# Half tiles from tile 57, one head folded by GpSimd, and three TensorE heads in the last row of a log-sum-exp kernel

## The chip, the cores and the metric

One core of a Trainium2 chip runs the program. The metric is the device time of one execution in microseconds (us), as the median of several runs; the profiled execution has a span from its first to its last instruction, which is about 2 us shorter than that time. All instants below are microseconds from the start of the span of the run named.

## The reference, cut to what matters

```python
def reference(x, bias):                       # x: 8 x 2048 x 2048 f32, bias: 8 x 256 f32
    x_heads = x.reshape(B, S, H, Dh).transpose(0, 2, 1, 3) + bias[None, :, None, :]
    x_tiled = np.repeat(x_heads, 2, axis=2)   # each row's result is stored twice
    mx = x_tiled.max(axis=-1, keepdims=True)
    return mx.squeeze(-1) + np.log(np.exp(x_tiled - mx).sum(axis=-1))
```

For each row and each of its 8 heads of 256 columns: add the head's bias, take the exponential, sum, take the logarithm.

## The kernel before

The input is read in 64 tiles of 2 MB; a tile holds two rows (k = 0, 1) of 2048 columns in each of 128 partitions, and nine tile buffers keep loads far ahead of the work. I call tile 62's two rows 62a and 62b. A head can be worked off in several ways, which a "mode" deals out:

- by TensorE and ScalarE ("pe" heads): a small matmul puts the bias into PSUM, a second one (identity times x, the "data matmul") adds x, and ScalarE takes exp and sums it in one instruction;
- by ScalarE and VectorE: exp of x alone, then VectorE multiplies by exp(bias) and sums;
- by GpSimd: it adds the bias before exp, or ("fold") multiplies by exp(bias) and halves the head three times, so that VectorE has only 32 columns left to sum.

In a mode, `pe` is the number of pe heads of a row, `g0` the first head to which GpSimd adds the bias (8: none), `fold` the number of folded heads. BULK, MIXED and PROMPT name modes of the code; PROMPT_F1 and PROMPT_F2 are PROMPT with one and two folded heads.

```python
MIXED = dict(pe=1, acc=1, g0=4, late=False, fold=0)
PROMPT = dict(pe=2, acc=2, g0=8, late=False, fold=0)
STAGES = [(0, (BULK,)), (50, (MIXED,)), (56, (MIXED, MIXED)), (61, (PROMPT, PROMPT)),
          (62, (PROMPT, PROMPT_F1)), (63, (PROMPT_F2, PROMPT))]   # two modes: the tile comes in halves
# ... cut ...
pairs = [pp.tile([P, 2 * MM], F32, name=f"pair{i}") for i in range(2)]   # PSUM, two banks each
ps = [p[:, c : c + MM] for p in pairs for c in (0, MM)]                  # four slots of one bank
# ... cut ...
def on_x(t, ins, after):
    known = [u for u in users[t] if u.ins.engine != ins.ins.engine]
    # ... cut: and the users of the same buffer's earlier tiles ...
    for u in known:
        if u not in after:
            tc.declare_no_dep(ins.ins, u.ins, reason="waited for by those it waits for")
    users[t].append(ins)
    return ins
# ... cut ...
            p = ps[n_ps[0] % len(ps)][:, 0 : (kb - ka) * n]   # put_bias: the next slot in turn
            n_ps[0] += 1
```

Slots are dealt in turn, two slots make one PSUM tile (a "pair"), and in the half-tile stages one half takes one slot. And `on_x` removes dependencies among the instructions that touch the same x tile. Waits are otherwise made by the build. ScalarE takes the pe heads of one half after it has issued the exp of the next half.

The softmax here doesn't subtract the row's maximum and nothing guards it: scores larger than these inputs give would overflow.

## Time and profile before

| the kernel before | |
|---|---|
| time | 327.51 us (327.42 to 327.84, 3 runs) |
| last piece of x has landed | 319.45 |
| VectorE's sums end | 322.00 |
| ScalarE's last head ends | 321.67 |
| span | 325.5 |

The way to read it is in the prediction. In all profile lines PE is TensorE, PEld its weight loads, DVE VectorE, ACT ScalarE and POOL GpSimd; L307 is line 307 of that run's kernel. The end of the load, in 1 us windows of the kernel before (the window, its length, busy time and number of instructions of PE, PEld, DVE, ACT and POOL, then the granted clock, that is the share of the full TensorE clock, the DMA share and GB/s):

```profile
319.00:320.00 1.00, 0.02 (x1) 0.00 (x0) 1.00 (x7) 1.00 (x3) 0.92 (x2) 1.00 0.99 295
320.00:321.00 1.00, 0.00 (x0) 0.00 (x0) 1.00 (x7) 1.00 (x6) 0.84 (x3) 1.00 0.45 152
```

TensorE is done at 319, VectorE and ScalarE are full: the tail belongs to them, and TensorE's clock happens to be 1.00 here.

### The profile page before, as it was taken

Reading aid. Unit: us, or ns where it says so; the run is one execution under the profiler, and the core shown is the slowest. Engines: PE = TensorE matmul, PEld = TensorE weight load, DVE = VectorE, ACT = ScalarE, POOL = GpSimd, SP = SyncE. Lnnn points to the kernel's source line nnn. Section 1 sums busy time; section 2 is a strip of 40 time slices with the busy share of each in tenths; the row PEclk is TensorE's granted clock in tenths of the full one; section 3 lists DMA queues with packets and bytes.
Section 4 is the critical chain, followed back from the end, with each engine's and each line's share of the span. In section 5 each row is a group of like instructions: output and inputs, shape, how many; then the busy total and the mean of one; then the engine's idle time right before and its main releaser. Section 6 shows DMA issues by size and latency. Waiting matters only on the chain.

```text
span 325.5 us, 2113 instructions
## 1 busy us (share of the span) xinstructions
PE 250.0 (77%) x541; PEld 86.9 (27%) x541; DVE 285.9 (88%) x320; ACT 264.3 (81%) x421; POOL 289.9 (89%) x88
## 2 busy tenths in 40 slices
PE   4478999499987888777879797889788455576792
PEld 1123333233322323223323232223223101122220
DVE  1006999999999999999898899989998999999995
ACT  1119999499978969888787978697879897799995
POOL 6999999799999999999999999999999999999713
PEclk9999999899979979998997989797979855555558
DMA  8999999999999999999999999999999999999994
GB/s 293 427 431 429 431 429 424 431 427 429 429 429 429 427 426 429 429 423 430 432 425 429 431 422 427 431 427 429 429 431 425 429 432 424 413 422 421 422 400 143
DMA packets 11806, 135.42 MB, mean 416 GB/s; under 512 B 1361, under 2 KB 1489, under 8 KB 2833
## 3 DMA queue, kind: packets, MB, share of 16 engines
q1 hardware_dynamic: 11696, 135.27, 98.6%
q8 instruction: 4, 0.07, 0.1%
q14 instruction: 8, 0.07, 0.0%
q10 hardware_dynamic: 2, 0.01, 0.0%
q0 software_dynamic: 96, 0.00, 0.0%
HBM read 134.23 MB, written 1.05 MB: 416 GB/s over the span
## 4 chain that ended last, share of the span: by engine, by line
DMA 48%; DVE 33%; ACT 8%; POOL 6%; PE 3%; issue 1%; SPq 0%; DVEq 0%
DMA xt<-in_x_dram 45%; DVE R L326 27%; ACT xt L307 6%; DVE xt L319 4%; POOL xt L301 4%; DMA b<-bparts 2%; PE pair L249 1%; PE one_ps L249 1%; DVE xt L342 1%; ACT xt L282 1%; DMA brow<-in_bias_dram 1%; ACT xt L267 1%; POOL brest L173 1%; POOL brest L171 1%; PE pair L203 0%
## 5 line engine op out<-in xcount | busy, mean ns | idle before, releaser
L301 POOL TENSOR_TENSOR xt<-xt,b_rep 128x2048 f32<-128x2048 f32 (+1 forms) x66 | 277.3, 4210 | 18.9 <-DMA xt<-in_x_dram 18.9
L326 DVE TENSOR_REDUCE R<-xt 128x14 f32<-128x3584 f32 (+1 forms) x56 | 208.1, 3716 | 2.6 <-ACT xt L307 0.9
L307 ACT ACTIVATE xt<-xt 128x2560 f32<-128x2560 f32 (+3 forms) x91 | 164.2, 1828 | 14.8 <-POOL xt L301 14.3
L249 PE MATMUL pair<-xt,ident 128*128 128x512 f32 x200 | 105.5, 654 | 0.0
L249 PE MATMUL one_ps<-xt,ident 128*128 128x512 f32 x100 | 61.0, 695 | 19.9 <-DMA xt<-in_x_dram 19.8
L267 ACT ACTIVATE xt<-pair 128x1024 f32<-128x1024 f32 x50 | 52.3, 1045 | 17.2 <-PE pair L249 15.8
L249 PEld LDWEIGHTS pair<-xt,ident 128*128 128x128 f32 x200 | 42.4, 212 | 56.0 <-issue 56.0
L319 DVE TENSOR_TENSOR xt<-xt,w_ps 128x512 f32<-128x512 f32 x50 | 34.0, 680 | 25.6 <-ACT xt L307 25.4
L233 PE MATMUL pair<-xt,ident 128*128 128x512 f32 (+1 forms) x44 | 34.0, 872 | 21.2 <-DMA xt<-in_x_dram 18.2
L260 ACT ACTIVATE xt<-one_ps 128x256 f32<-128x256 f32 x100 | 37.7, 394 | 8.1 <-PE one_ps L249 8.1
L203 PE MATMUL one_ps<-b,ones 3*128 3x512 bf16 x50 | 19.0, 381 | 17.9 <-ACT xt L260 11.8
L203 PEld LDWEIGHTS <-ones 3*128 3x128 bf16 x150 | 12.5, 92 | 65.7 <-issue 59.7
L203 PE MATMUL pair<-b,ones 3*128 3x512 bf16 x100 | 29.9, 378 | 0.0
L249 PEld LDWEIGHTS one_ps<-xt,ident 128*128 128x128 f32 x100 | 15.6, 197 | 41.3 <-DMA xt<-in_x_dram 34.1
L260 ACT ACTIVATION_READ_ACCUMULATOR xt<-one_ps 128x1 f32 x100 | 22.1, 221 | 0.0
L342 DVE CUSTOM_DVE_ANT_0 xt<-xt,one_ps 128x256 f32<-128x256 f32 x50 | 19.1, 414 | 0.3 <-ACT xt L307 0.3
L233 PEld LDWEIGHTS pair<-xt,ident 128*128 128x128 f32 x44 | 10.4, 294 | 29.6 <-DMA xt<-in_x_dram 19.7
L342 DVE CUSTOM_DVE_ANT_0 xt<-xt,w_ps 128x256 f32<-128x256 f32 x45 | 17.5, 417 | 0.0
L282 ACT ACTIVATE xt<-pair 128x256 f32<-128x256 f32 x34 | 12.5, 374 | 0.1
L326 DVE TENSOR_REDUCE R_last<-xt 128x4 f32<-128x1024 f32 x10 | 12.1, 1214 | 0.0
L218 PE MATMUL pair<-b,ones 3*128 3x512 bf16 (+1 forms) x22 | 10.2, 465 | 1.1 <-ACT xt L267 1.1
L358 POOL TENSOR_TENSOR xt<-xt,w_sb 128x256 f32<-128x256 f32 (+1 forms) x2 | 2.1, 1026 | 8.7 <-ACT xt L307 8.5
(38 smaller groups left out, 55.9 us busy)
## 6 DMA issues: line engine op xcount, KB each, us to landing
xt<-in_x_dram SPq DMA_DIRECT2D x56, 2048.0 KB, 29.9
xt<-in_x_dram SPq DMA_DIRECT2D x14, 1024.0 KB, 21.0
xt<-in_x_dram SPq DMA_DIRECT2D x5, 256.0 KB, 11.4
out_dram<-res SPq DMA_DIRECT2D x1, 896.0 KB, 7.3
xt<-in_x_dram SPq DMA_DIRECT2D x2, 384.0 KB, 16.5
out_dram<-res_last SPq DMA_DIRECT2D x1, 128.0 KB, 1.7
b<-bparts POOLq DMA_DIRECT2D x3, 1.5 KB, 6.5
brow<-in_bias_dram ACTq DMA_DIRECT2D x1, 8.0 KB
```

What stands on the lines that cost most here:

```text
L203: nc.tensor.matmul(p, lhsT=ones3, rhs=each_row(b3, h * Dh, Dh, K), start=True, stop=False,)
L218: nc.tensor.matmul(p, lhsT=ones3, rhs=each_row(b3, 0, n, kb - ka), start=True, stop=False,)
L233: mm = nc.tensor.matmul(p, lhsT=ident, rhs=xts[t % NBUF][:, ka:kb, 0:n], start=False, stop=True,)
L249: mm = nc.tensor.matmul(p, lhsT=ident, rhs=xts[t % NBUF][:, :, h * Dh : (h + 1) * Dh], start=False, stop=True,)
L260: act = nc.scalar.activation(out=xts[t % NBUF][:, k, 0:Dh], in_=got[0][:, k * Dh : (k + 1) * Dh], func=ACT.Exp, accum_out=sums[:, k, 0:1],)
L267: act = nc.scalar.activation(out=xts[t % NBUF][:, :, Dh : m["pe"] * Dh].rearrange("p k (h j) -> p h k j", j=Dh), in_=got[-1].rearrange("p ...
L282: act = nc.scalar.activation(out=xts[t % NBUF][:, k, c : c + Dh], in_=p[:, c : c + Dh], func=ACT.Exp, accum_out=sums[:, k, h : h + 1],)
L301: add = nc.gpsimd.tensor_tensor(out=v, in0=v, in1=each_row(b_rep, c - G0, D - c, k1 - k0), op=ALU.add)
L307: return on_x(t, nc.scalar.activation(out=v, in_=v, func=ACT.Exp), [after])
L319: mul = nc.vector.tensor_tensor(out=f, in0=f, in1=each_row(w_ps, m["pe"] * Dh - W0, n, k1 - k0), op=ALU.mult,)
L326: red = nc.vector.tensor_reduce(out=sums[:, k0:k1, h0:H], in_=v.rearrange("p k (h j) -> p k h j", j=Dh), op=ALU.add, axis=mybir.AxisListTy ...
L342: ttr = nc.vector.tensor_tensor_reduce(out=v, in0=v, in1=w, scale=1.0, scalar=0.0, op0=ALU.mult, op1=ALU.add, accum_out=dst,)
```

## The change

The intent: fewer, cheaper half tiles (from 57 instead of 56, with GpSimd folding one head instead of adding a bias to four), BULK kept up to tile 53 instead of 49, less ScalarE work in tile 62, and in the very last row one head more for TensorE, so that VectorE has five sums in that row instead of six. The third TensorE head is loaded next to last, so that the last piece is one head of 128 KB.

```diff
-PROMPT = dict(pe=2, acc=2, g0=8, late=False, fold=0)
+SINGLE_F1 = dict(pe=1, acc=1, g0=8, late=False, fold=1)
+TRIPLE = dict(pe=3, acc=3, g0=8, late=False, fold=0)
 # ... cut ...
 STAGES = [
     (0, (BULK,)),
-    (50, (MIXED,)),
-    (56, (MIXED, MIXED)),
-    (61, (PROMPT, PROMPT)),
-    (62, (PROMPT, PROMPT_F1)),
-    (63, (PROMPT_F2, PROMPT)),
+    (54, (MIXED,)),
+    (57, (PROMPT_F1, PROMPT_F1)),
+    (62, (SINGLE_F1, SINGLE_F1)),
+    (63, (PROMPT_F2, TRIPLE)),
 ]
 LAST_COLS = [
     [(0, 512), (1280, 2048), (512, 1280)],
-    [(0, 512), (512, 1024), (1024, 1536), (1536, 2048)],
+    [(0, 512), (768, 1280), (1280, 1792), (512, 768), (1792, 2048)],
 ]
```

The rest of the diff (cut) lets a row have more than 512 TensorE columns, and lets heads go with any piece. One order of instructions changes with it: ScalarE now takes the two TensorE heads of 63a before the exps of 63b (`if c0 == 0: flush(for_pe)`), where the kernel before left them to the end.

More of the change, by code (lines that the diff above doesn't have):

```diff
@@ L211, in put_bias, with add_x @@
         n = m["pe"] * Dh
-        step = MM // n
+        rows = min(k1 - k0, max(MM // n, 1))
         got = []
-        for ka in range(k0, k1, step):
-            kb = min(ka + step, k1)
-            p = ps[n_ps[0] % len(ps)][:, 0 : (kb - ka) * n]
-            n_ps[0] += 1
-            nc.tensor.matmul(
-                p,
-                lhsT=ones3,
-                rhs=each_row(b3, 0, n, kb - ka),
-                start=True,
-                stop=False,
-            )
-            got.append((ka, kb, p))
-        return got
-    def add_x(m, t, k0, got):
-        n = m["pe"] * Dh
-        rows = []
-        for ka, kb, p in got:
+        for k in range(k0, k1, rows):
+            for c in range(0, n, MM):
+                w = min(n - c, MM)
+                p = ps[n_ps[0] % len(ps)][:, 0 : rows * w]
+                n_ps[0] += 1
+                nc.tensor.matmul(
+                    p,
+                    lhsT=ones3,
+                    rhs=each_row(b3, c, w, rows),
+                    start=True,
+                    stop=False,
+                )
+                got.append((k, k + rows, c, w, p))
+        return got
+    def add_x(m, t, k0, c0, c1, got):
+        heads = []
+        for ka, kb, c, w, p in got:
+            if not c0 <= c < c1:
+                continue
             mm = nc.tensor.matmul(
@@ L235, in add_x @@
                 lhsT=ident,
-                rhs=xts[t % NBUF][:, ka:kb, 0:n],
+                rhs=xts[t % NBUF][:, ka:kb, c : c + w],
                 start=False,
@@ L239, in add_x @@
             )
-            on_x(t, mm, [loads[t, k0, 0]])
-            rows += [(p[:, k * n : (k + 1) * n], mm) for k in range(kb - ka)]
-        return rows
+            on_x(t, mm, [loads[t, k0, c0]])
+            for i in range(0, (kb - ka) * w, Dh):
+                k, cw = divmod(i, w)
+                heads.append((ka + k, (c + cw) // Dh, p[:, i : i + Dh], mm))
+        return heads
     def late_heads(m, t, got, sums):
@@ L276, in late_heads, with sum_biased @@
         return pe_part
-    def sum_biased(m, t, k, p, mm, sums):
-        for h in range(m["pe"]):
-            c = h * Dh
-            act = nc.scalar.activation(
-                out=xts[t % NBUF][:, k, c : c + Dh],
-                in_=p[:, c : c + Dh],
-                func=ACT.Exp,
-                accum_out=sums[:, k, h : h + 1],
-            )
-            last_uses[t].append(on_x(t, act, [mm]))
+    def sum_biased(t, k, h, p, mm, sums):
+        act = nc.scalar.activation(
+            out=xts[t % NBUF][:, k, h * Dh : (h + 1) * Dh],
+            in_=p,
+            func=ACT.Exp,
+            accum_out=sums[:, k, h : h + 1],
+        )
+        last_uses[t].append(on_x(t, act, [mm]))
     def each_row(src, c, n, k_rows):
@@ L452, with pe_part @@
             add = None
+            heads = []
             if c0 == 0:
-                if m["late"]:
-                    pe_part = late_heads(m, t, bias_there, sums)
-                else:
-                    got = add_x(m, t, k0, bias_there)
+                bias_here = bias_there
+            if m["late"]:
+                pe_part = late_heads(m, t, bias_here, sums)
+            else:
+                heads = add_x(m, t, k0, c0, c1, bias_here)
+                def pe_part(t=t, heads=heads, sums=sums):
+                    for k, h, p, mm in heads:
+                        sum_biased(t, k, h, p, mm, sums)
+            if c0 == 0:
                 if next_units and not m["late"]:
@@ L461 @@
                     add = g_add(m, t, k0, k1)
-            if c0 == 0 and (t < T - 1 or k0 == 0):
-                flush(for_pool)
+                if t < T - 1 or k0 == 0:
+                    flush(for_pool)
             if t == T_PROMPT and c0 == 0:
@@ L475 @@
                     for_pool.append(fold(t, k0, hf, h1, sums, done))
-            if c0 == 0 and (t < T - 1 or k0 == 0):
+            if c0 == 0:
                 flush(for_pe)
@@ L493, in pool_part @@
                     load(t + NBUF)
-            if not m["late"]:
-                def pe_part(t=t, m=m, got=got, k0=k0, k1=k1, sums=sums):
-                    for k in range(k0, k1):
-                        sum_biased(m, t, k, *got[k - k0], sums)
             for_pool.append(pool_part)
-            if c0 == 0:
-                if m["g0"] < H:
-                    pe_part()
-                    if m["late"]:
-                        bias_there = put_bias(*next_units.pop(0))
-                else:
-                    for_pe.append(pe_part)
+            if m["g0"] < H:
+                pe_part()
+                if m["late"]:
+                    bias_there = put_bias(*next_units.pop(0))
+            elif heads:
+                for_pe.append(pe_part)
         fb, at = divmod(t - 2, NBLK)
```

## The prediction

> **What bounds the kernel now.** I read the page's shares and slices first, then the chain of waits for the last 30 us, then the timelines of TensorE and ScalarE for the same stretch.
>
> ```profile
> PEclk9999999899979979998997989797979855555558
> DMA  8999999999999999999999999999999999999994
> GB/s 293 427 431 429 431 429 424 431 427 429 429 429 429 427 426 429 429 423 430 432 425 429 431 422 427 431 427 429 429 431 425 429 432 424 413 422 421 422 400 143
> ```
>
> The DMA row is full in every slice but the first and the last: the kernel streams 134.2 MB at about 429 GB/s, and that stream sets the time. The chain's total (DMA 48%, VectorE 33%) must not be read as "VectorE is a third of the bound": it follows VectorE only through the early tiles, where VectorE works off the start-up backlog while transfers run full beside it. The completion events of the trace give the pace: a 2 MB tile lands every 4.90 us, a half tile every 2.48 us, the first half of tile 62 at 311.74, its second at 314.24, the seven pieces of tile 63 from 314.91 to 319.45. Nothing in the change moves these bytes. So what it can touch is what comes after the last landings: 319.45 to the span's end, 325.5, about 6.1 us. This is how that end looks in the chain of waits:
>
> ```profile
> 294.41 19.82 DMA xt<-in_x_dram
> ...
> 314.26 1.48 ACT xt L307
> 315.74 1.46 ACT xt L282 x8
> 317.20 1.47 ACT xt L307 x2
> ...
> 318.69 0.42 DVE xt L342
> ...
> 321.86 0.14 DVE R_last L372
> 322.00 0.14 issue
> 322.14 0.32 PE tpair L408
> 322.45 0.02 issue
> 322.48 0.39 ACT res_last L414
> ```
>
> The columns are start, length, what. From the landing of tile 62's second half, ScalarE works without a gap: its exp (1.48), four bias heads (1.46), the two exps of tile 63's first row (1.47). Then VectorE does nine multiply-and-sum instructions, 3.09 us at 0.343 us each, and one small reduction, to 322.00. Transpose, Ln, store and the end take the other 3.5 us and stay. ScalarE's own last bias head ends at 321.67, so it is only 0.33 us off the path.
>
> TensorE looks idle enough on average, but not in clock. PEclk is 5 from 258 us to 316 us. The timeline of TensorE shows what this costs:
>
> ```profile
> 304.33 1.22 PE L233 MATMUL pair<-xt,ident 128*128 128x256 f32 x2 [0.94 <-DMA xt<-in_x_dram]
> ...
> 309.36 2.08 PE L233 MATMUL pair<-xt,ident 128*128 128x512 f32 x2
> 311.37 0.60 PE L218 MATMUL pair<-b,ones 3*128 3x512 bf16 x1
> 311.90 2.08 PE L233 MATMUL pair<-xt,ident 128*128 128x512 f32 x2
> ...
> 316.52 1.13 PE L233 MATMUL pair<-xt,ident 128*128 128x512 f32 x2
> ```
>
> A pair of heads of one row (512 columns) takes 2.08 us at half clock and 1.13 us at full. With its bias matmul the period is 2.54 us (309.36 to 311.90), just more than the 2.48 us of a half tile.
>
> **What the Trainium skill says.** "TensorE: Matmul & The Clock Gate", Part 1: the array's clock is halved by default, and released only after a busy window of about 3.4 us that runs free of the kernel. The trace agrees: the granted clock is 0.5 or 1.0 alone, and the slow pieces last 3.41 us or multiples of it. The trace adds a grade: the window 309.07 to 312.49, in which the data matmuls filled 2.67 of 3.41 us, did not release the clock, the next, with 2.94, did (at 315.9). "DMA: Bandwidth & Descriptors", "Where 436 GB/s comes from", sets the ceiling at 435 GB/s and says that HBM binds near 358; the trace's 429 agrees with the first and not with the second. The same page, "Why small descriptors are slow (HBM only)", has a fixed cost per packet; here 2048-byte packets took 84 ns, and the last store's 1024-byte ones 46 ns, so two of those cost 8 ns more. "ScalarE: Activation LUTs", "Step-by-step: what each stage is for", has 0.833 ns per element: 1536 elements then are 1.28 us, and the trace has one such exp every 1.37 us with its start.
>
> **The change part by part.**
>
> 1. Tiles 50 to 53 go from MIXED back to BULK. VectorE per tile: 0.60 + 3.89 = 4.5 us against 4.35 us (six times 0.344 and a 2.28 us reduction), both under 4.90. Hidden: 0.
>
> 2. Tile 56 is loaded whole again, and 57 to 61 change from MIXED halves to PROMPT_F1 halves. Per half, before: GpSimd 2.33 us (add of 1024), ScalarE 2.3 us, VectorE 3 x 0.344 + 1.22 = 2.25. After: GpSimd 2.05 us (the fold in the trace, 315.82 to 317.87), ScalarE 1.37 + 2 x 0.365 = 2.1, VectorE 5 x 0.344 + 0.19 = 1.9. All under 2.48 and lower than before. There is a bump at the change-over: tile 56 lands at 284.4, its add lasts 4.56 us, its second exp comes at 289.1, and ScalarE is then behind by two halves. At 0.38 us regained per half (2.48 - 2.1) it is level again at tile 62, by my step-by-step addition at 311.7 us, VectorE at about 313.4. It is just in time, and the stream does not notice, since loads were issued 20 us earlier. Hidden: 0.
>
> 3. Tile 62 goes from PROMPT to SINGLE_F1: one bias head, seven exps, one folded. ScalarE per half: 1.37 + 256 x 0.833 ns + 0.365 = 1.95. VectorE: six instructions and a reduction, 2.25.
>
> 4. Row 1 of tile 63: three heads by TensorE, five by VectorE instead of six; heads 2 and 7 come as separate 128 KB pieces, head 7 last. Smaller packets: 2 x 8 packets per engine x 4 ns = 0.06 us later.
>
> The end of ScalarE and VectorE, added up from 314.26 with these durations: ScalarE exp of 62b 1.60 to 315.85, two heads to 316.58, two exps of 768 to 318.04 (before 318.67), two heads of row 0 to 318.77, exps of 512, 512 and 256 to 320.10. VectorE: 62a from 313.5 to 315.8, 62b from 316.0 (exp end) to 318.3, then nine instructions and a reduction, 3.31 us: 321.6. Before 322.0. So these two **gain 0.4 us**: the removed sixth instruction of the last row is paid for by the sixth in tile 62's second half.
>
> TensorE now. Tile 62 has only 256 columns per half, 1.22 of 2.48 us, so nothing in it would release the clock. At half clock: 62b 314.26 to 315.4, bias to 315.95, row 0 of tile 63 to 317.96 (its data lay there since 314.91), two bias matmuls to 318.83, heads 0 and 1 of row 1 (landed 317.54) to 320.9, head 2 another 1.2 us, to 322.1. ScalarE's last head then runs 322.1 to 322.55, against 322.0 for the end of the sums before: **a loss of 0.55 us**. At full clock the same work takes half and ends under ScalarE's exps; then VectorE's 321.6 stands.
>
> So the sum is -0.4 or +0.55 us, by the clock. I stepped the TensorE work through 3.41 us windows at forty phases, with release at 2.75 to 2.85 us of data matmul and fall below 2.2 to 2.33 us of all work (read from the windows before, as the rule above): the clock is low at the end in two thirds to four fifths of them. Weighted: about +0.3 us.
>
> **The rivals.** (a) The clock is at full rate at the end: PROMPT_F1 fills TensorE (2.54 of 2.48 us), which before released the clock after nine us of it (306.8 to 315.9). For: five tiles of it. Against: at full clock the load is only 1.5 of 2.48 us, and windows with 2.1 to 2.3 us of work were followed by a fall in the bulk stage; and tile 62 lies between. Time: 327.1. (b) TensorE at half clock becomes the bound of the tail: as worked out, 328.1, my main case. (c) The change-over backlog is not worked off by tile 62, because folds on GpSimd and sums on VectorE slow each other, or ScalarE's starts cost more: each tenth of a microsecond per half makes one microsecond at tile 62, and the end goes to 328.5 to 329. Against: VectorE's instructions kept 0.343 us in the trace while GpSimd folded (316 to 321). (d) The extra pieces or the store of the first seven batches (896 KB, 314.3 to 321.64) get in the way of the last loads: it is issued after the piece eight earlier has landed, so now 0.7 us later than before; that helps by at most 0.1 us.
>
> **Range and chances.** From 327.51: 327.1 with a quarter to a third of the weight, 328.1 with most of the rest, so 327.8. Run-to-run spread of the kernel before is 0.4 us; with (c) the range is 326.9 to 328.6. Two per cent is 6.5 us, more than the whole tail, and a lost stream would need an engine above 2.48 us per half for long: same 0.98.
>
> **What would show it right or wrong.** DMA at about 429 GB/s up to slice 38 and the last piece landing within 0.3 us of 319.5 (step 0). VectorE's last small reduction at about 321.6 (sum of the tail). The data matmul of head 2 ending near 322 at clock 0.5, with the transpose waiting for ScalarE (main case), or near 320 at clock 1.0, with the transpose waiting for VectorE (rival a). ScalarE level with the landings at tile 62 (step 2). I am wrong if the stream itself shows a gap between 285 and 312, if the tail is bound by neither, or if the time moves by over a microsecond.

## The result and the profile after

The changed kernel takes **328.63 us** (328.42 to 328.90, 4 runs) against 327.67 us (327.42 to 327.94) of the kernel before in the same rounds: 0.96 us slower, ratio 1.0030, interval 1.0012 to 1.0047.

The stream did what was expected. The slices of the page of the changed kernel:

```profile
PEclk9999999879997997997997979798998997559657
DMA  8999999999999999999999999999999999999993
GB/s 296 428 431 431 429 429 422 429 427 431 425 427 431 427 424 431 423 433 426 426 431 427 427 428 423 427 433 423 427 433 424 425 433 419 421 421 421 419 384 97
```

The DMA row is as full as before, and by the completion events the last piece lands at 319.30, 0.15 us earlier than before. So the loss lies behind it. PEclk shows one difference: in the half-tile stage the clock is no longer low throughout (a 9 and a 6 among the 5s), but it is low towards the end, where it was high before. The chain of waits of the changed kernel, for the same stretch as in the prediction:

```profile
294.09 20.02 DMA xt<-in_x_dram
...
314.15 1.22 PE pair L237 x2
315.37 0.54 PE pair L220
315.90 2.02 PE pair L237 x2
317.92 0.02 issue
317.94 0.47 ACT xt L286 x2
318.42 1.46 ACT xt L311 x2
319.88 0.73 ACT xt L286 x4
320.61 0.53 ACT xt L311
...
321.16 0.42 DVE xt L346
...
322.96 0.14 DVE R_last L376
323.11 0.14 issue
323.24 0.32 PE tpair L412
```

Before, the chain went from the landing of 62b straight to ScalarE. ScalarE's exp of 62b still starts at once (314.13), but the chain now leads over three TensorE pieces: 62b's data matmul, the bias matmul of 63a, and 63a's data matmul, 3.8 us at half clock. ScalarE waits for them before its next head (0.47), and its exps of tile 63 come after it. The timeline of ScalarE says which head that is:

```profile
315.73 0.37 ACT L286 ACTIVATE xt<-pair 128x256 f32<-128x256 f32 x1
...
317.94 0.38 ACT L286 ACTIVATE xt<-pair 128x256 f32<-128x256 f32 x1 [1.76 <-PE pair L237]
```

The head at 315.73 is 62a's, the one at 317.94 is 62b's: tile 62 has one TensorE head per half. 62b's own data matmul had ended at 315.37. ScalarE stood 1.76 us for a matmul whose result it did not read.

The built program shows why. TensorE counts up a semaphore, and 62b's head waits for a value of it (read from a build of each kernel; no trace holds these values):

```
kernel           62b's head waits for   that value is reached by
changed          375                    63a's data matmul
e1_nodep         373                    62b's own data matmul
e2_align         377                    the bias matmul of 63b's third head
```

62b and 63a stand in the two banks of the same pair. The build keeps dependencies by PSUM tile, here a whole pair, and 63a's matmul is issued before 62b's head is, so the head waits for it. In the kernel before, the two halves that share a pair belong to the same tile, and there `on_x` happens to declare this dependency away. Starting the half tiles at 57 instead of 56 shifts the slots by one, and pairs now straddle two tiles.

### The profile page after: what moved, and what is told of

Its sections match the earlier page's. It is cut to its first block, busy times and chain, and to the rows that moved or that the text cites. A ratio compares the mean times of both kernels' runs of the same rounds, so it can differ in the third digit from the quotient of the medians.

```text
span 326.6 us, 2184 instructions
## 1 busy us (share of the span) xinstructions
PE 260.4 (80%) x565; PEld 90.3 (28%) x565; DVE 283.7 (87%) x306; ACT 263.6 (81%) x425; POOL 290.6 (89%) x123
## 4 chain that ended last, share of the span: by engine, by line
DMA 47%; DVE 34%; ACT 6%; POOL 6%; PE 5%; issue 1%; SPq 0%; DVEq 0%
DMA xt<-in_x_dram 44%; DVE R L330 29%; ACT xt L311 5%; DVE xt L323 4%; POOL xt L305 4%; DMA b<-bparts 2%; PE pair L255 2%; PE pair L237 1%; PE one_ps L255 1%; DMA brow<-in_bias_dram 1%; ACT xt L273 1%; ACT xt L286 1%; DVE xt L346 1%; POOL brest L171 1%; POOL brest L173 1%
## 5 line engine op out<-in xcount | busy, mean ns | idle before, releaser
L305 POOL TENSOR_TENSOR xt<-xt,b_rep 128x2048 f32<-128x2048 f32 x57 | 258.8, 4543 | 18.9 <-DMA xt<-in_x_dram 18.9
L330 DVE TENSOR_REDUCE R<-xt 128x14 f32<-128x3584 f32 (+1 forms) x56 | 214.5, 3830 | 1.9
L311 ACT ACTIVATE xt<-xt 128x2560 f32<-128x2560 f32 (+5 forms) x77 | 158.3, 2066 | 11.2 <-POOL xt L305 10.8
L255 PE MATMUL pair<-xt,ident 128*128 128x512 f32 x216 | 115.7, 663 | 0.0
L255 PE MATMUL one_ps<-xt,ident 128*128 128x512 f32 x108 | 65.8, 693 | 20.3 <-DMA xt<-in_x_dram 20.3
L237 PE MATMUL pair<-xt,ident 128*128 128x512 f32 (+1 forms) x36 | 28.6, 896 | 8.9 <-DMA xt<-in_x_dram 4.5
L346 DVE CUSTOM_DVE_ANT_0 xt<-xt,w_ps 128x256 f32<-128x256 f32 x61 | 22.4, 413 | 1.2 <-ACT xt L311 1.1
L370 POOL TENSOR_TENSOR xt<-xt 128x128 f32<-128x128 f32 (+3 forms) x39 | 13.9, 356 | 3.1
L362 POOL TENSOR_TENSOR xt<-xt,w_sb 128x256 f32<-128x256 f32 (+1 forms) x13 | 10.0, 773 | 6.6 <-ACT xt L311 6.0
L346 DVE CUSTOM_DVE_ANT_0 xt<-xt,one_ps 128x256 f32<-128x256 f32 x27 | 10.5, 411 | 0.9 <-ACT xt L311 0.9
```

The costliest lines, as they stand in the source:

```text
L237: mm = nc.tensor.matmul(p, lhsT=ident, rhs=xts[t % NBUF][:, ka:kb, c : c + w], start=False, stop=True,)
L255: mm = nc.tensor.matmul(p, lhsT=ident, rhs=xts[t % NBUF][:, :, h * Dh : (h + 1) * Dh], start=False, stop=True,)
L305: add = nc.gpsimd.tensor_tensor(out=v, in0=v, in1=each_row(b_rep, c - G0, D - c, k1 - k0), op=ALU.add)
L311: return on_x(t, nc.scalar.activation(out=v, in_=v, func=ACT.Exp), [after])
L330: red = nc.vector.tensor_reduce(out=sums[:, k0:k1, h0:H], in_=v.rearrange("p k (h j) -> p k h j", j=Dh), op=ALU.add, axis=mybir.AxisListTy ...
L346: ttr = nc.vector.tensor_tensor_reduce(out=v, in0=v, in1=w, scale=1.0, scalar=0.0, op0=ALU.mult, op1=ALU.add, accum_out=dst,)
```

## The experiments

**Theory A:** ScalarE is held by a false wait through the shared PSUM pair, and TensorE's half clock makes that wait long. **Rivals:** B, TensorE at half clock bounds the tail by itself; C, VectorE's additional sum in 62b; D, the later start of the half tiles and its backlog.

| run | time, us | before in its rounds | ratio (interval) |
|---|---|---|---|
| e1_nodep | 327.44 | 327.35 | 1.0000 (0.9988 to 1.0013) |
| e2_align | 329.33 | 327.35 | 1.0060 (1.0047 to 1.0072) |
| e3_before57 | 328.27 | 327.35 | 1.0034 (1.0021 to 1.0047) |
| e4_before58 | 328.37 | 327.35 | 1.0032 (1.0019 to 1.0046) |
| e5_warm | 326.96 | 327.47 | 0.9985 (0.9974 to 0.9997) |
| e6_nodep_warm | 326.94 | 327.47 | 0.9987 (0.9975 to 0.9999) |
| e7_before_odd | 328.15 | 327.47 | 1.0034 (1.0014 to 1.0053) |
| e8_nodep_2h | 327.49 | 327.47 | 0.9999 (0.9987 to 1.0011) |
| e9_before57_nodep | 327.93 | 327.45 | 1.0015 (1.0003 to 1.0027) |
| e10_nodep_62p | 328.34 | 327.45 | 1.0016 (1.0002 to 1.0031) |
| e11_before_warm | 327.44 | 327.45 | 1.0000 (0.9987 to 1.0013) |

All eleven gave correct results; the medians are of 5 runs (6 for e7 and e10).

### e1_nodep: the wait removed

```diff
             on_x(t, mm, [loads[t, k0, c0]])
+            x_mms.append(mm)
...
+        for other in x_mms:
+            if other is not mm and x_mms.index(other) > x_mms.index(mm):
+                tc.declare_no_dep(act.ins, other.ins, reason="another bank")
         last_uses[t].append(on_x(t, act, [mm]))
```

The head's wait for its own matmul stays.

> The changed kernel, with one false dependency declared away: a bias head's exp on ScalarE no longer waits for a later piece's data matmul that writes the other bank of the same PSUM pair. Theory A (that wait holds ScalarE 1.76 us, from 316.2 to 317.9 of the span): the head of tile 62's second half starts at about 316.1, the sums end near 322.0 instead of 323.1, time falls by 0.9 to 1.1 us to 327.5 to 327.7. Rival B (TensorE at half clock bounds the tail by itself, the wait is only where it shows): the end stays within 0.3 us of 328.6. Rival C (the added sixth sum per half of tile 62 loads VectorE): no change, 328.6.

Measured: 327.44 us, level with the kernel before. That is 1.19 us less than the changed kernel's median, or 0.87 us less if each is taken against the kernel before in its own rounds (328.63 - 327.67 = 0.96 and 327.44 - 327.35 = 0.09). Theory A's number holds. The chain of waits of this run:

```profile
314.09 1.22 PE pair L238 x2
315.32 0.53 PE pair L221
315.85 2.01 PE pair L238 x2
317.86 0.75 PE pair L221 x2
318.61 2.02 PE pair L238 x2
320.62 0.02 issue
320.65 0.84 ACT xt L288 x4
```

62b's head now starts at 316.03, as soon as ScalarE is free for it:

```profile
316.03 0.38 ACT L288 ACTIVATE xt<-pair 128x256 f32<-128x256 f32 x1
```

The tail is TensorE's at half clock, from the landing of 62b straight through, and the sums end with ScalarE's third head at 321.98. So B is real as a floor (it is why nothing is gained on the kernel before), but it was not what made the loss. C falls: VectorE's extra sum is still there.

### e2_align: slots shifted back

```diff
         n = m["pe"] * Dh
+        if k0 == 0 and k1 == 1 and n_ps[0] % 2:
+            n_ps[0] += 1
```

> The changed kernel with one PSUM slot skipped at tile 57, so that the two halves of a tile share a pair again, as in the kernel before. Theory A in its exact form (a head waits for whatever was last issued into its pair before it): tile 62's second head now shares its pair with nothing of tile 63's first row, but the third head of the last row (256 columns) falls on the other bank, so by the built program it waits for that bias matmul, which follows the data matmul of 63a: start at 318.5 instead of 317.9, so 0.5 to 0.7 us slower than the changed kernel: 329.1 to 329.4. Rival A' (only a pair that straddles two tiles hurts, aligned ones don't): 327.6. B and C: 328.6.

Measured: 329.33 us, 1.98 us over the kernel before in its rounds. This is the strange number that only the exact form of A expects: aligning the pairs makes it worse, since 63b with three heads takes two slots and the second falls into the pair of 62b. The timeline of ScalarE in this run:

```profile
318.62 0.39 ACT L288 ACTIVATE xt<-pair 128x256 f32<-128x256 f32 x1 [2.50 <-PE pair L222]
```

62b's head waits 2.50 us, for a bias matmul of the last row. Neither B nor C has a reason for that.

### e3_before57 and e4_before58: the start of the half tiles alone

In the kernel before, `(56, (MIXED, MIXED))` becomes `(57, ...)` in one run and `(58, ...)` in the other.

> The kernel before with half tiles from tile 57 instead of 56 and nothing else, which shifts its PSUM slots by one, so that pairs straddle two tiles. Theory A: the heads of tile 62's second half wait for the data matmul of tile 63's first row: 1.2 us later at full clock (317.65 instead of 316.4), 2.5 us at half clock; time 328.7 to 330.0. Rivals B and C, and 'the start of the half tiles costs nothing by itself': 327.7 within 0.3.

> The kernel before with half tiles from tile 58: pairs aligned again, two tiles fewer in halves. Theory A: 327.7 within 0.3, as the kernel before. Rival D (it is the later start of the half tiles, and the backlog at the change-over, that costs): slower than with 57, over 328.7.

Measured: 328.27 and 328.37 us. Neither lies in a range that I had given: e3 is slower, as A says, but by less than A's least (328.7), and e4 is above A's 328.0 and below D's 328.7. With 58 the pairs are aligned, and yet it is 1.0 us slower than the kernel before. So the later start costs something by itself, which A does not give; the direction is D's. The chain of e4 goes from the last whole tile to the end on VectorE:

```profile
289.26 4.55 POOL xt L301
...
293.83 1.92 ACT xt L307
...
295.77 2.29 DVE R_last L326
```

From there it does not leave VectorE until the last sum. A whole tile's late GpSimd add leaves VectorE behind, and MIXED halves (one every 2.15 us on VectorE, where the prediction had summed 2.25, per 2.48 us of load) regain too little per half. So in the kernel before, starting the halves at 56 and not at 58 is worth a microsecond for a reason of its own, and e3 may mix two causes.

### e9_before57_nodep: splitting e3

The kernel of e3 with the declaration of e1.

> Splits the run of the kernel before with half tiles from 57 (0.9 us slower) into its two possible causes: false wait or backlog of the change-over. The same kernel with the false dependency declared away. If the false wait was the cause (theory A): back to 327.4 to 327.7. If the backlog on VectorE was (as the run with 58 shows one): stays at 328.1 to 328.4.

Measured: 327.93 us, with single runs from 327.49 to 328.51, while e3's ran from 328.18 to 329.38. It lies between the two expectations, and the ranges overlap: by the medians the false wait makes perhaps a third of a microsecond of e3's 0.9. The two profiled executions (328.18 us for e3, 327.55 us for e9) say more. In e3's, 61b's first head stands for 62a's data matmul:

```profile
314.21 0.39 ACT L282 ACTIVATE xt<-pair 128x256 f32<-128x256 f32 x1 [0.86 <-PE pair L233]
```

In e9's, the same head starts at 313.22, and the chain stays on VectorE from the last whole tile to the last sum, as in e4. The sums end at 322.68 in e3's and 322.07 in e9's (322.00 in the kernel before). In this pair the wait makes 0.6 us, and the backlog alone leaves about 0.1. The other runs of e9, up to 328.51, have no profile, so how the medians divide stays open.

### e7_before_odd: the false wait put into the kernel before

```diff
         n = m["pe"] * Dh
+        if k0 == 0 and k1 == 1 and n_ps[0] % 2 == 0:
+            n_ps[0] += 1
         step = MM // n
```

> The kernel before with one PSUM slot skipped at tile 56, nothing else: same stages, same loads, pairs now straddle tiles. Theory A: heads of 61b and 62b wait for the next tile's data matmul, 0.9 to 2.5 us of ScalarE idle in all near 313 to 318, time 328.3 to 329.8. Rival (slots don't matter; the half-tile start and its backlog do): 327.4 within 0.2.

Measured: 328.15 us (327.86 to 330.08), 0.68 us slower than the kernel before, with the same stages and the same loads. Direction as A expects, size just below its range: in the profiled execution (328.09 us) the clock went to full at 313.74, so only one wait was long, that of 61b's heads for 62a's data matmul:

```profile
314.04 0.39 ACT L284 ACTIVATE xt<-pair 128x256 f32<-128x256 f32 x1 [0.67 <-PE pair L235]
```

This is the cleanest single-cause test of the slots: nothing but one skipped PSUM slot. The runs of 328.85 and 330.08 us have no profile.

### e5_warm, e6_nodep_warm and e11_before_warm: the clock

In the changed kernel (e5), in e1's (e6) and in the kernel before (e11), TensorE gets matmuls of constants whose result nobody reads, in the idle time of tiles 59 to 62a.

```diff
+WARM = {
+    **{(t, k): (128, 128) for t in (59, 60, 61) for k in (0, 1)},
+    (62, 0): (128,) * 4,
+}
...
+                for n in WARM.get((t, k0), ()):
+                    nc.tensor.matmul(tpair[:, 1, 0], lhsT=ident, rhs=w_sb[:, 0:n],
+                                     start=True, stop=True)
```

> The changed kernel, false wait kept, with idle TensorE time of tiles 59 to 62a filled by matmuls of constants into an unused half of a PSUM bank (result not read), so that the clock gate stays open. Theory A with the half clock as its second factor: at full clock 63a's data matmul ends at 316.1 to 316.3, when ScalarE gets to that head anyway; the false wait costs under 0.2 us, the sums end at 321.4 to 321.7 with VectorE, time 327.0 within 0.3. If the false wait alone were the cause at any clock: 328.6. If the filler itself delays the data matmuls, TensorE stays at half clock and is late: over 329.

> Both: the false dependency declared away and the clock held up by filler. Theory A: within 0.2 us of the run with filler alone, 326.9 to 327.1, VectorE last at 321.4 to 321.7; faster than the kernel before by 0.3 to 0.5 us. Rival B (half clock alone bounds): the same number, but then the run with filler and without the declaration equals it as well, and the run with the declaration alone would not have gained.

> Control: the kernel before with the same filler matmuls. Its tail is VectorE's, with TensorE 0.3 us or more off the path, so the filler should be worth nothing: 327.4 within 0.2. If the filler made any kernel faster by 0.4 us, the gain of the changed kernel with filler (326.96) would not show the clock as its cause: then 327.0.

Measured: 326.96, 326.94 and 327.44 us. With the clock at full from 294.65 to 321.96 the changed kernel, false wait and all, beats the kernel before by 0.5 us. TensorE and ScalarE in e5:

```profile
315.34 1.12 PE L241 MATMUL pair<-xt,ident 128*128 128x512 f32 x2
```

```profile
316.50 0.38 ACT L290 ACTIVATE xt<-pair 128x256 f32<-128x256 f32 x1
```

63a's data matmul ends at 316.46 instead of 317.92, and 62b's head follows at 316.50, 0.16 us after ScalarE was free for it. VectorE ends the sums at 321.66. Removing the false wait as well (e6) adds nothing; the two medians are 0.02 us apart. So the loss needs both, the false wait and the half clock: with the wait away (e1) or with the clock up (e5) it is gone. The control e11 gains nothing from filler, so filler is no general gift; it pays where TensorE is on the path. (The kernel before had the full clock in its tail anyway, from 315.90; with filler it has it from 310.90.)

### e8_nodep_2h: the three heads of the last row

On top of e1, the last row is back to two TensorE heads and four pieces of 512 columns.

> The changed kernel with the false dependency declared away and the last row back to two TensorE heads and four equal pieces. At half clock the third head (0.85 us of matmul, 0.35 us of bias) is gone from TensorE's chain and a sixth sum (0.34 us) is back on VectorE: sums end at 321.9 to 322.0 by VectorE instead of 321.98 by ScalarE: 327.4 within 0.2, no difference to the run with three heads. If the three heads are worth their sum: 0.3 us slower, 327.8.

Measured: 327.49 us against e1's 327.44. The centrepiece of the change, one VectorE sum fewer in the last row, is worth nothing here: VectorE ends the sums at 321.76 in this run, and ScalarE, held by TensorE, at 321.98 in e1; that is 2.4 and 2.7 us behind the last landing of their runs. The clock differs too: in this run's profile it went to full at 319.79, in e1's at 321.68. Whether the third head pays at full clock (on top of e5 or e6) was not tested.

### e10_nodep_62p: tile 62 with two TensorE heads

On top of e1, the line `(62, (SINGLE_F1, SINGLE_F1))` is gone, so tile 62 is PROMPT_F1.

> The changed kernel with the false dependency declared away and tile 62 with two TensorE heads per half instead of one. Two ways by the clock of TensorE: if it stays at half, 62b's data matmul is 0.85 us longer on TensorE's chain and the sums end at 322.8, 328.2; if twelve halves of two heads release the clock before 316, as they did in the kernel before, VectorE ends at 321.5 and the time is 327.0. The granted clock at 314 to 321 decides, and a wide spread of the runs would show both.

Measured: 327.17, 327.18, 328.31, 328.36, 328.51 and 328.53 us. One kernel on one chip has two times, 1.2 us apart. The profiled execution is one of the two short ones: its clock went to full at 318.04, and the last row's matmuls were short from there. The two levels lie 0.2 and 0.1 to 0.3 us above the two that were expected for the two clocks. That the clock makes the difference is not shown: the longer runs have no profile, and the mean clocks of whole runs (0.889 and 0.900 for the short ones, 0.881 to 0.890 for the long) do not separate them.

## Why the prediction was wrong

By its own steps:

- **The stream stays** and the first two parts are hidden: right. The last landing was expected within 0.3 us of 319.5 and came at 319.30; DMA moved 421 GB/s from 285 to 312 in both kernels. ScalarE was level with the load at 62a (its exp began at 311.60, the half landed at 311.58), as the step-by-step addition had it.
- **The clock is low at the end**, in two thirds of the phases or more: right in the profiled execution; the share was not tested. It was 0.5 from 311.44 to 321.68, and both data matmuls of 62b and 63a took what I had put down for half clock (62b 314.15 to 315.37, 63a 315.90 to 317.92; predicted 314.26 to 315.4 and 315.95 to 317.96). The rule behind the forecast does not hold, though, so some of this is luck. In the kernel before itself, a window with 2.15 us of all work (145.23 to 148.64) was not followed by a fall; and 2.94 us of data matmuls, which released the clock there, did not do so in e10 (307.80 to 311.22), while 2.72 us did in e8 (207.14 to 210.55).
- **The sum of ScalarE: this is the step that failed.** "ScalarE exp of 62b 1.60 to 315.85, two heads to 316.58": the first head was free at 315.73, the second stood until 317.94. I added up durations in program order and took for granted that a head waits for its own matmul. So "two exps of 768 to 318.04" became 319.9, and VectorE's 321.6 became 323.1. It was VectorE that ended last, by way of the ScalarE exps, and not TensorE by way of ScalarE's last head, as my main case said: TensorE's last data matmul ended at 321.52. ScalarE's last head ended only 0.05 us before VectorE, at 323.05, so the changed order of its last heads cannot have cost more than that.
- **The loss of 0.55 us from TensorE** at half clock: right in mechanism, too large. With the false wait taken away (e1) that chain is the tail, and it ends at 321.98 where I had 322.55: 62b landed 0.19 us earlier there than in the trace I had worked from, and the third head's matmul took some 0.85 instead of 1.2 us behind its predecessor. Against the kernel before, what is left of this term is 0.09 us by the medians, ratio 1.0000 (e1). So it is luck that the time went up as forecast: the loss that I had summed is not the one that came.
- **The gain of 0.4 us** at full clock: right. With filler, VectorE ends at 321.66 (predicted 321.6) and the time is 0.5 us below the kernel before, in a kernel that has filler added (rival (a): 327.1; measured 326.96).
- **Rival (c)**, the backlog, did not happen in the changed kernel: VectorE stood idle before 312.84. It does happen with MIXED halves (e4), so it was the right thing to fear.

So the forecast of 327.8 was 0.83 us low, and the measured median lies 0.03 us above the range. The whole miss, and more, is one wait of 1.76 us that I had not seen, though it could be read before any run: from the slot order in the code, or from the semaphore values of the built program.

What remains open: how e3 divides between wait and backlog outside the two profiled executions, the clock in e10's longer runs, and the third head at full clock.

**The best version** is the changed kernel with filler matmuls, 326.96 us, or with the dependency declared away as well, 326.94 us. Both are 0.5 us below the kernel before in the same rounds (the intervals allow 0.03 to 0.85), which itself is about 1 us below the changed kernel.

## What to carry to other kernels

An engine waits for what the build thinks it needs: where two independent things share one PSUM tile, a later write to one half can hold a reader of the other, and shifting a stage by one tile can switch that on. When you move work between buffers that are dealt in turn, compare the awaited semaphore values in the built programs before and after, not only the order of instructions. And when a tail is a chain through several engines, work it out for each clock that TensorE may have, since a light load, put there to help, may keep the clock low: in the profiled executions it came back at 321.68 with the light tile 62 (e1) and at 318.04 with two heads there (e10).

## What the Trainium skill lacked or had wrong

- "Perfetto Trace Analysis", "Optimizing Tensor Performance", under "Matmuls", advises that independent matmul groups rotate through different PSUM banks so that the evacuation of one overlaps the matmuls of the next. It doesn't say that this can fail in the build: with two banks in one PSUM tile, ScalarE's read of one bank waited 1.76 us (2.50 us in e2) for a matmul into the other; declaring it away was worth 0.9 to 1.2 us.
- "TensorE: Matmul & The Clock Gate", Part 1, says that the clock is released after a busy window, but not how busy. The time of data matmuls in a window of 3.41 us does not tell it here: 2.94 us released the clock in the kernel before and not in e10, and 2.72 us did in e8. With tile 62 lightened the clock was at half for 10.24 us up to 321.68 (it had fallen at 311.44, just before 62a landed); with filler (1.16 us of it in 62a) it stayed at full.
- The same page's Part 1 says that the phase of the window makes cold matmuls vary from run to run. It does not say that a kernel can show this as two separate times; e10 has 327.17 and 327.18 us beside 328.31 to 328.53, and the clock is the only cause that I found for it; it is not shown, since the longer runs have no profile.
- "DMA: Bandwidth & Descriptors", "Where 436 GB/s comes from", says that for transfers between HBM and SBUF the HBM side, about 358 GB/s, binds. With one core running, the changed kernel moved 419 to 433 GB/s in 37 of 40 slices of its span, near the 435 GB/s that the page gives for the fabric. Only this sentence is wrong for one core: a few lines above, the same page has a measured 425 GB/s for a core alone, and the 358 for two cores that stream at once.
